# An early split of branch A's prompt columns, the sample rows' output and norm on 128 partitions, and filler matmuls in the first pauses

## The chip, the cores and the metric

The kernel runs on one core of one Trainium2 chip. A core has a matrix engine (TensorE, written PE in the profile, with its weight loads as PEld), a vector engine (VectorE, DVE), an engine for pointwise functions (ScalarE, ACT), a general engine (GpSimd, POOL) and a queue that starts transfers (SyncE, SP). The engines run side by side and wait for one another only where one needs what another makes. The time is that of the device for one execution, in microseconds (us); less is better.

## The reference

One step of a decoder layer with two gated branches, for a prompt of 512 rows and 32 sample rows (8 sequences of 4), all in float32 with 1024 features:

```python
shift, scale, gate = jnp.split(jax.nn.silu(c) @ w_cond + b_cond, 3, axis=-1)
h = x * (1 + scale[:, None]) + shift[:, None]
# one projection of h gives q, k, v, z of both branches and the two gates
ya = o_a.reshape(bsz, seq, A_OUT_WIDTH).astype(dtype) * jax.nn.silu(za)
yb = ob.reshape(bsz, seq, B_WIDTH).astype(dtype) * jax.nn.silu(zb)
merged = jax.nn.sigmoid(ga) * (ya @ w_branch_a) + jax.nn.sigmoid(gb) * (yb @ w_branch_b)
r = (ALPHA * x + gate[:, None] * (merged @ w_out)).astype(jnp.float32)
mu = jnp.mean(r, axis=-1, keepdims=True)
var = jnp.mean(jnp.square(r - mu), axis=-1, keepdims=True)
y = ((r - mu) * lax.rsqrt(var + LN_EPS)).astype(dtype) * ln_g + ln_b
```

Branch A is softmax attention over dilated windows (o_a, 512 features). Its sample rows also read 2048 cached keys and values. Branch B is a gated delta rule (o_b, 1024 features). The outputs are also the new caches and states.

## The kernel before

**Layout.** Activations are kept with features on the 128 partitions and the 544 rows (512 prompt, then 32 sample) along the free axis. A product is made in two halves of 272 columns, so the first half holds prompt rows only, and the second holds 240 prompt rows and the 32 sample rows. A float32 product is made of three fast ones: each operand is split into a rounded part (hi, an ACT copy to the type fp32r) and the rest (lo, a DVE subtraction), and hi*hi, hi*lo and lo*hi are added up in one PSUM bank.

**Order of the work.** The body doesn't issue instructions; it records them (`Recorder.add`). `Recorder.schedule` (lines 457 to 701) then makes one order for each engine: it goes through the work with a table of costs, and an engine takes the ready instruction of the lowest rank, among equals the one that was recorded first. Line 616 lets PE stay up to 1 us with matmuls of one shape before it changes to another shape that is ready. Line 625 holds an engine back from a PSUM bank until the engine that used it last is through with its work there. A field `at` keeps an instruction from being taken before that moment of the plan. `emit` (line 725) issues everything in the order found, so that every instruction of the profile carries line 725, and groups are told apart by the names of their tiles. On the chip each engine keeps its order whatever happens; a wait in it holds up all that stands behind.

**Threads.** The parts of the body are generators with ranks (lines 735 to 775). `stream` (line 1030, rank 9) runs the list `jobs` of matrix products in order; each job has its weights loaded five jobs ahead, split one job ahead, and `evac` takes each half out of PSUM. Its operations on other engines than PE get rank -1 (line 276), ahead of the rest. The samples' work has rank 1.

**Front** (lines 893 to 1017). `cond_block` (line 929) makes scale (part 1) and shift (part 0) from w_cond, for one or two of the eight 128-feature chunks: 16 narrow matmuls with `cs`, a DVE copy Y, then matmuls with the selection `selc`; both results lie in one PSUM bank. The copies x1 of the scaled input and the first three product sums (`sums`) follow chunk by chunk, as the loads of wc, xT and W3 come in.

**Before the change's middle place** (lines 2183 to 2215). The jobs are gate and branch products of B (m = 0 to 7), then the gates ga0 to ga6 (`EARLY_A` = 7). Beside them runs `samples`: the delta rule of the samples, then their attention over the cache (`sample_attention`, pieces of 128x1024 multiplied and reduced on DVE, tile `kv` into `od`; then the matmuls `pO`, lines 1847 to 1858, `om`, and a transpose into `os_`). When all threads are over, `gate_samples` (line 1875) multiplies `os_` by the gate and copies it into columns 512 to 543 of the four tiles `ya`. Lines 2224 to 2228 then split each `ya` into `yah` and `yal`. `ya` and `yah` share a tag of five buffers in the pool `keep`; `yal` takes a buffer of the tag "o" in `opool`, which has nine, and which the gates ga2 to ga6 and the eight `ybh` of branch B use as well. Then come the branch products `branch_job("ga", m)` with `merge_after(m)`, which split the merged rows into `mhi` and `mlo`. After the fourth of them w_out is loaded.

**End** (lines 2270 to 2360). For each half n of the 1024 output columns, `product_out` makes blocks tt = 0 to 3 of 128 prompt rows (24 matmuls of 512 columns; two lots of 24 with 256 columns for tt = 3). DVE takes the product out with the gate `gp`, adds the scaled x (`load_x`, two buffers) and makes the statistics `bn`. With n = 1, `norm_out` follows: aggregate, square root on ACT, three passes of `scalar_tensor_tensor` and two stores. Between the halves stands `samples_out` (line 2319): the samples' product is made with four column quarters of 256 on four groups of 32 partitions, but then brought onto partitions 0 to 31 for the addition and the norm over 1024 columns.

Of the kernel before, what the change touches and what calls it, by code (L numbers as in the profile page):

```python
# [19 lines left out]
D = 1024  # L20
# [21 lines left out]
TOGETHER = ((0,), (1, 2), (3, 4), (5, 6), (7,))  # L42
CHUNKS = ((0, 1), (1, 1), (2, 2), (4, 2), (6, 2))
# [34 lines left out]
def shape_constants():  # L78

    p = np.arange(128)  # L80
    b4, i4, h8 = p // 32, p // 8 % 4, p % 8
    blk = {}
    blk["ident"] = np.eye(128)
    blk["selc"] = (p[:, None] % 32 == np.arange(9)[None, :])
    tok = np.arange(2 * NS)
    blk["selg"] = (p[:, None] % 32 == 1 + tok[None, :] % NS // 4)
    blk["triu"] = (p[:, None] <= p[None, :])
    same = p[:, None] // 4 == p[None, :] // 4
    blk["btri"] = same & (p[:, None] <= p[None, :])
    blk["bones"] = same  # L90
    blk["low16"] = np.where(p[:, None] % 32 >= 16, -1.0, 0.0)
    blk["strict4"] = same & (p[:, None] < p[None, :])
    blk["dmask"] = np.where(p[:, None] <= p[None, :], 0.0, -BIG)
    blk["dmask_s"] = np.where(same & (p[:, None] <= p[None, :]), 0.0, -BIG)
    blk["bmask"] = (p[:, None] % 32 // 4 == np.arange(8)[None, :])
    blk["hmask"] = (p[:, None] % 4 == np.arange(4)[None, :])
    sab = np.zeros((128, 4, 4))
    for h4 in range(4):
        for g in range(2):
            sab[4 * g + h4::16, h4, g] = 1.0  # L100
            sab[8 + 4 * g + h4::16, h4, 2 + g] = 1.0
# [3 lines left out]
    for names in (("ident", "selc", "selg", "low16", "dmask"), ("selab", "sel16", "triu", "btri", "bones"),  # L105
                  ("strict4", "dmask_s", "bmask"), ("hmask",)):
# [671 lines left out]
def body(ctx, tc, io):  # L778
# [114 lines left out]
    with ExitStack() as fctx:  # L893
# [35 lines left out]
        def cond_block(part, at, m, other):  # L929

            ps, wc, w = pb_() if other else pg(), pieces[part, at], 128 * m
            rec.rank = -1
            with rec.together():
                for k in range(KT):
                    q = k % 4
                    pe.matmul(ps[32 * q:32 * q + 32, 0:w].rearrange("p (a b) -> p a b", b=128), cs[:, k, :], wc[:, :, k, :],
                              start=(k < 4), stop=(k >= 4), tile_position=(0, 32 * q))
# [3 lines left out]
            with rec.together():  # L941
                for i in range(m):
                    pe.matmul(pv[:, i, 0:9], Y[:, 128 * i:128 * i + 128], C("selc"), start=True, stop=True)
            rec.rank = 0
# [930 lines left out]
    def gate_samples():  # L1875
        ve.scalar_tensor_tensor(os_, os_, 0.5, szs, op0=OP.mult, op1=OP.mult)
        for j in range(4):
            ve.tensor_copy(ya[j][:, SEQ:], os_[:, j])
# [330 lines left out]
    jobs += [gate_job("ga", m) for m in range(EARLY_A)]  # L2209
    threads.add(finish_early(), 0)  # L2210
    threads.add(samples(), 1)
    threads.add(after_b(), 0)
    threads.add(stream(len(jobs)), 9)
# [10 lines left out]
    for j in range(4):  # L2224
        yah[j] = keep.tile([128, NT], F32R, name="yah", tag="ya", bufs=5)
        se.activation(yah[j], ya[j], AF.Copy)
        yal[j] = op.tile([128, NT], F32R, name="yal", tag="o")
        ve.tensor_sub(yal[j], ya[j], yah[j].bitcast(F32))
# [56 lines left out]
    r = [o1.tile([128, D], F32, name=f"r{tt}") for tt in range(5)]  # L2285
# [12 lines left out]
    def load_x(tt, n):  # L2298
        rows = slice(0, 128) if tt < 4 else slice(0, 32)
        xr = o2.tile([128, 512], F32, name="xr")  # L2300
        sp.dma_start(xr[rows], io["x"][128 * tt:128 * tt + 128 if tt < 4 else NT, 512 * n:512 * n + 512])
        se.activation(xr[rows], xr[rows], AF.Copy, scale=ALPHA)
        return xr[rows]

    def norm_out(tt, mv=None):
        rows = slice(0, 128) if tt < 4 else slice(0, 32)
        q = r[tt][rows]
        if mv is None:
            mv = o2.tile([128, 4], F32, name="mv")[rows]
            ve.bn_aggr(mv[:, 0:2], bn[tt][rows].rearrange("p a b -> p (a b)"))  # L2310
        se.activation(mv[:, 2:3], mv[:, 1:2], AF.Sqrt, bias=eps5[rows, 0:1])
        ve.scalar_tensor_tensor(q, q, mv[:, 0:1], lng[rows], op0=OP.subtract, op1=OP.mult)
        ve.reciprocal(mv[:, 2:3], mv[:, 2:3])
        out = io["y_p"][128 * tt:128 * tt + 128] if tt < 4 else io["y_s"]
        for w in (slice(0, 512), slice(512, 1024)):
            ve.scalar_tensor_tensor(q[:, w], q[:, w], mv[:, 2:3], lnb[rows, w], op0=OP.mult, op1=OP.add)
            sp.dma_start(out[:, w], q[:, w])

    def samples_out():
        xr = [load_x(4, n) for n in range(2)]  # L2320
# [73 lines left out]
def lay_out(x):  # L2394
# [13 lines left out]
        "const_s": CONST[3],  # L2408
        "x": rows,
# [61 lines left out]
```

## Time and profile before

| | |
|---|---|
| median of three runs | 898.17 us (897.95, 898.17, 901.1) |
| profiled execution | 902.66 us |
| its span, first to last instruction | 900.9 us |
| mean granted clock of TensorE | 0.993 |
| memory read, written | 218.20 MB, 103.97 MB |
| costliest groups | matmuls of hhi and hlo with the weights, 4080 of 128x272: 1201.5 us of (overlapping) busy time |

The profile is of one execution. A row in order of time has the start and the length in us, the engine, the operation, out<-in with partitions x elements, the count, and in brackets how long the engine had been idle before it and what ended that. A row of a group has the count, then the busy time in us and the mean of one in ns, then the idle time before. Matmuls overlap: the pace is the distance of their starts, not their length.

### The profile page before, as it was taken

Reading aid. Unit: us, or ns where it says so; the run is one execution under the profiler, and the core shown is the slowest. Engines: PE = TensorE matmul, PEld = TensorE weight load, DVE = VectorE, ACT = ScalarE, POOL = GpSimd, SP = SyncE. Lnnn points to the kernel's source line nnn. Section 1 sums busy time; section 2 is a strip of 40 time slices with the busy share of each in tenths; the row PEclk is TensorE's granted clock in tenths of the full one; section 3 lists DMA queues with packets and bytes.
Section 4 is the critical chain, followed back from the end, with each engine's and each line's share of the span. In section 5 each row is a group of like instructions: output and inputs, shape, how many; then the busy total and the mean of one; then the engine's idle time right before and its main releaser. Section 6 shows DMA issues by size and latency. Waiting matters only on the chain.

```text
span 900.9 us, 20727 instructions
## 1 busy us (share of the span) xinstructions
PE 873.6 (97%) x8178; PEld 822.2 (91%) x8178; DVE 650.8 (72%) x1341; ACT 449.9 (50%) x1076; POOL 74.1 (8%) x173
## 2 busy tenths in 40 slices
PE   6999999999999999999999999999999999989995
PEld 5899999898899999899999899897999999989884
DVE  3675447643379998399987658366889698978568
ACT  3555478733478834579734565642542222324331
POOL 0120011100101200012101101020010000001000
PEclk9999999999999999999999999999999999999998
DMA  9865785785868798878889556559869799985953
GB/s 348 322 212 172 235 277 174 249 275 165 293 200 302 234 293 276 309 245 261 274 287 286 188 193 214 177 180 317 315 224 382 270 408 411 352 305 170 366 187 122
DMA packets 106189, 235.84 MB, mean 262 GB/s; under 512 B 30199, under 2 KB 61633, under 8 KB 103405
## 3 DMA queue, kind: packets, MB, share of 16 engines
q1 hardware_dynamic: 106092, 234.53, 76.3%
q8 instruction: 64, 1.05, 0.5%
q14 instruction: 33, 0.26, 0.1%
HBM read 218.20 MB, written 103.97 MB: 358 GB/s over the span
## 4 chain that ended last, share of the span: by engine, by line
PE 83%; DVE 7%; ACT 4%; DMA 4%; issue 1%; SPq 1%; DVEq 0%; ACTq 0%
PE pp L725 63%; PE pg L725 9%; PE pd L725 7%; PE pb L725 4%; DVE slab L725 1%; ACT L725 1%; DMA S<-in_state_delta 1%; DVE lo L725 1%; DMA rbo<-dO 1%; DVE acc L725 1%; DVE r L725 1%; DMA slab<-in_bias_s 1%; SPq L725 1%; DMA out_kv_s<-in_cache 1%; DMA wc<-in_w_cb 1%
## 5 line engine op out<-in xcount | busy, mean ns | idle before, releaser
L725 PE MATMUL pp<-hhi,hi 128*128 128x272 f32 x1360 | 400.8, 295 | 1.0 <-DVE zt L725 0.5
L725 PE MATMUL pp<-hlo,hi 128*128 128x272 f32 x1360 | 400.8, 295 | 0.0
L725 PE MATMUL pp<-hhi,lo 128*128 128x272 f32 x1360 | 399.9, 294 | 0.0
L725 PEld LDWEIGHTS pp<-hhi,hi 128*128 128x128 f32 x1360 | 256.8, 189 | 4.8 <-issue 2.2
L725 PEld LDWEIGHTS pp<-hhi,lo 128*128 128x128 f32 x1360 | 256.6, 189 | 3.8 <-issue 2.7
L725 PEld LDWEIGHTS pp<-hlo,hi 128*128 128x128 f32 x1360 | 257.1, 189 | 2.8 <-issue 1.7
L725 ACT ACTIVATE hi<-wt 128x1024 fp32r<-128x1024 f32 (+1 forms) x101 | 103.6, 1026 | 160.3 <-PE pp L725 135.1
L725 DVE TENSOR_TENSOR lo<-wt,hi 128x1024 fp32r<-128x1024 f32 (+1 forms) x101 | 119.0, 1178 | 81.3 <-ACT hi L725 74.5
L725 DVE SCALAR_TENSOR_TENSOR acc<-ext,cw,acc 128x568 f32<-128x568 f32 x72 | 57.9, 804 | 0.8 <-ACT acc L725 0.2
L725 DVE TENSOR_TENSOR slab<-slab 128x512 f32<-128x512 f32 (+1 forms) x66 | 43.3, 670 | 10.0 <-DMA slab<-qd 4.4
L725 ACT ACT_TABLE_LOAD x32 | 41.1, 1283 | 5.2 <-PE pp L725 3.0
L725 DVE TENSOR_REDUCE slab<-slab 128x8 f32<-128x512 f32 (+2 forms) x66 | 42.8, 660 | 0.3
L725 ACT ACTIVATE zt<-pp 128x272 f32<-128x272 f32 x48 | 18.8, 391 | 40.6 <-PE pp L725 38.4
L725 ACT ACTIVATE P<-P,st 128x256 f32<-128x256 f32 (+1 forms) x64 | 31.3, 493 | 12.7 <-DVE st L725 12.6
L725 PE MATMUL pp<-ybh,lo 128*128 128x272 f32 x128 | 37.0, 289 | 0.0
L725 PE MATMUL pp<-ybl,hi 128*128 128x272 f32 x128 | 37.0, 289 | 0.0
L725 PE MATMUL pp<-ybh,hi 128*128 128x272 f32 x128 | 36.8, 288 | 0.0
L725 POOL COPY cx<-ext 128x3 f32<-128x3 f32 (+1 forms) x48 | 23.9, 527 | 114.5 <-ACT ext L725 109.9
L725 DVE CUSTOM_DVE_ANT_0 P<-pg,bias 128x256 f32<-128x256 f32 (+1 forms) x64 | 23.1, 401 | 9.3 <-PE pg L725 9.1
L725 ACT ACTIVATE spare<-pp 128x272 f32<-128x272 f32 (+1 forms) x32 | 16.2, 505 | 19.8 <-PE pp L725 18.2
L725 PEld LDWEIGHTS pp<-ybh,hi 128*128 128x128 f32 x128 | 24.2, 189 | 0.1
L725 PEld LDWEIGHTS pp<-ybl,hi 128*128 128x128 f32 x128 | 24.1, 188 | 0.1
(402 smaller groups left out, 1574.5 us busy)
## 6 DMA issues: line engine op xcount, KB each, us to landing
out_kv_s<-in_cache SPq DMA_DIRECT2D x144, 512.0 KB
wt<-in_w_in SPq DMA_DIRECT2D x85, 512.0 KB
out_kv_s<-in_cache SPq DMA_DIRECT2D x24, 496.0 KB
wc<-in_w_cb SPq DMA_DIRECT2D x16, 512.0 KB
slab<-in_ks SPq DMA_DIRECT2D x32, 256.0 KB
slab<-in_vs SPq DMA_DIRECT2D x32, 256.0 KB
kv<-in_ks SPq DMA_DIRECT2D x16, 512.0 KB
kv<-in_vs SPq DMA_DIRECT2D x16, 512.0 KB
```

Source lines behind the costliest of these rows:

```text
L725: getattr(real[x.engine], x.name)(*map(arg, x.args), **{k: arg(v) for k, v in x.kw.items()})
```

## The change

It has three parts, and each keeps what is computed.

- *Front.* `cond_block` of chunk 0, part 1, gets 8 matmuls of ones by ones ahead of its 16, 2 right behind them and 5 behind the selection matmuls, written to the unused columns 384 to 511 of the block's bank. The block of chunk 1 may not start before 9.9 us of the plan.
- *Middle.* A thread `split_prompt_a` of rank 0 splits columns 0 to 511 of `ya` when job `jobs[-4]` (ga3) is over, one tile every 6 us of the plan. `gate_samples` splits the 32 sample columns straight into `yah` and `yal`, with 4 ACT copies and 4 DVE subtractions of 128x32, and lines 2224 to 2228 go.
- *End.* `samples_out` keeps the four quarters on their 128 partitions: product, addition and statistics are 256 wide. The mean and the variance over the four quarters come from two matmuls with `quarter` (0.25 where two partitions hold the same row). `ln_g` and `ln_b` are loaded a second time in that layout (`lns`, eight small transfers), x and y_s are moved in four pieces each.

```diff
+IDLE = (8, 2, 5)
...
+    blk["quarter"] = np.where(p[:, None] % 32 == p[None, :] % 32, 0.25, 0.0)
...
             ps, wc, w = pb_() if other else pg(), pieces[part, at], 128 * m
+            idle = IDLE if (part, at) == (1, 0) else (0, 0, 0)
             rec.rank = -1
+
+            def turn_over(n):
+                for _ in range(n):
+                    pe.matmul(ps[:, 384:512], ones, ones, start=True, stop=True)
+
+            turn_over(idle[0])
             with rec.together():
                 for k in range(KT):
                     q = k % 4
                     pe.matmul(ps[32 * q:32 * q + 32, 0:w].rearrange("p (a b) -> p a b", b=128), cs[:, k, :], wc[:, :, k, :],
-                              start=(k < 4), stop=(k >= 4), tile_position=(0, 32 * q))
+                              start=(k < 4), stop=(k >= 4), tile_position=(0, 32 * q)).at = 9.9 * ((part, at) == (1, 1))
+                turn_over(idle[1])
...
                 for i in range(m):
                     pe.matmul(pv[:, i, 0:9], Y[:, 128 * i:128 * i + 128], C("selc"), start=True, stop=True)
+                turn_over(idle[2])
...
     def gate_samples():
         ve.scalar_tensor_tensor(os_, os_, 0.5, szs, op0=OP.mult, op1=OP.mult)
         for j in range(4):
-            ve.tensor_copy(ya[j][:, SEQ:], os_[:, j])
+            se.activation(yah[j][:, SEQ:], os_[:, j], AF.Copy)
+            ve.tensor_sub(yal[j][:, SEQ:], os_[:, j], yah[j][:, SEQ:].bitcast(F32))
+
+    def split_prompt_a():
+        yield split_at.over
+        for j in range(4):
+            yah[j] = keep.tile([128, NT], F32R, name="yah", tag="ya", bufs=5)
+            se.activation(yah[j][:, :SEQ], ya[j][:, :SEQ], AF.Copy)
+            yal[j] = op.tile([128, NT], F32R, name="yal", tag="o")
+            ve.tensor_sub(yal[j][:, :SEQ], ya[j][:, :SEQ], yah[j][:, :SEQ].bitcast(F32))
+            yield 6.0
...
     jobs += [gate_job("ga", m) for m in range(EARLY_A)]
+    split_at = jobs[-4]
     threads.add(finish_early(), 0)
     threads.add(samples(), 1)
     threads.add(after_b(), 0)
+    threads.add(split_prompt_a(), 0)
...
-    for j in range(4):
-        yah[j] = keep.tile([128, NT], F32R, name="yah", tag="ya", bufs=5)
-        se.activation(yah[j], ya[j], AF.Copy)
-        yal[j] = op.tile([128, NT], F32R, name="yal", tag="o")
-        ve.tensor_sub(yal[j], ya[j], yah[j].bitcast(F32))
...
+    lns = o1.tile([128, 2, 256], F32, name="lns")
+    for i, n in enumerate(("ln_g", "ln_b")):
+        for q in range(4):
+            sp.dma_start(lns[32 * q:32 * q + 32, i], io[n][:, 256 * q:256 * q + 256].to_broadcast([32, 256]))
+    quarter = o1.tile([128, 128], F32, name="quarter")
+    sp.dma_start(quarter, io["const_q"])
...
     def samples_out():
-        xr = [load_x(4, n) for n in range(2)]
+        xr = o1.tile([128, 256], F32, name="xs")
+        for b in range(4):
+            sp.dma_start(xr[32 * b:32 * b + 32], io["x"][SEQ:NT, 256 * b:256 * b + 256])
+        se.activation(xr, xr, AF.Copy, scale=ALPHA)
...
-        q = r[4][0:32]
+        q = r[4]
+        ve.scalar_tensor_tensor(q, po[:, 0:256], 0.5, gs, op0=OP.mult, op1=OP.mult)
+        ve.tensor_add(q, q, xr)
+        ve.bn_stats(bn[4][:, 0, :], q)
+        mv = o2.tile([128, 4], F32, name="mv")
+        ve.bn_aggr(mv[:, 0:2], bn[4][:, 0, :])
+        pm = pd()
+        pe.matmul(pm[:, 0:1], quarter, mv[:, 0:1], start=True, stop=True)
+        se.activation(mv[:, 2:3], pm[:, 0:1], AF.Square, bias=mv[:, 0:1], scale=-1.0)
+        ve.tensor_add(mv[:, 1:2], mv[:, 1:2], mv[:, 2:3])
+        pe.matmul(pm[:, 1:2], quarter, mv[:, 1:2], start=True, stop=True)
+        se.activation(mv[:, 3:4], pm[:, 1:2], AF.Sqrt, bias=eps5)
+        ve.tensor_copy(mv[:, 2:3], pm[:, 0:1])
+        ve.scalar_tensor_tensor(q, q, mv[:, 2:3], lns[:, 0], op0=OP.subtract, op1=OP.mult)
+        ve.reciprocal(mv[:, 3:4], mv[:, 3:4])
+        ve.scalar_tensor_tensor(q, q, mv[:, 3:4], lns[:, 1], op0=OP.mult, op1=OP.add)
         for b in range(4):
-            rows = slice(32 * b, 32 * b + 32)
-            ve.scalar_tensor_tensor(q[:, 256 * b:256 * b + 256], po[rows, 0:256], 0.5, gs[rows], op0=OP.mult, op1=OP.mult)
-        for n in range(2):
-            w = slice(512 * n, 512 * n + 512)
-            ve.tensor_add(q[:, w], q[:, w], xr[n])
-            ve.bn_stats(bn[4][0:32, n, :], q[:, w])
-        norm_out(4)
+            sp.dma_start(io["y_s"][:, 256 * b:256 * b + 256], q[32 * b:32 * b + 32])
```

More of the change, by code (lines that the diff above doesn't have):

```diff
@@ L105, in shape_constants @@
     for names in (("ident", "selc", "selg", "low16", "dmask"), ("selab", "sel16", "triu", "btri", "bones"),
-                  ("strict4", "dmask_s", "bmask"), ("hmask",)):
+                  ("strict4", "dmask_s", "bmask"), ("hmask",), ("quarter",)):
         at = 0
@@ L2284, in body @@
     ve.memset(eps5, LN_EPS)
-    r = [o1.tile([128, D], F32, name=f"r{tt}") for tt in range(5)]
+    lns = o1.tile([128, 2, 256], F32, name="lns")
[4 more added lines that the diff above has]
+    sp.dma_start(quarter, io["const_q"])
+    r = [o1.tile([128, D if tt < 4 else 256], F32, name=f"r{tt}") for tt in range(5)]
     bn = [o1.tile([128, 4 if tt == 3 else 2, 6], F32, name=f"bn{tt}") for tt in range(5)]
@@ L2298, in load_x @@
     def load_x(tt, n):
-        rows = slice(0, 128) if tt < 4 else slice(0, 32)
         xr = o2.tile([128, 512], F32, name="xr")
-        sp.dma_start(xr[rows], io["x"][128 * tt:128 * tt + 128 if tt < 4 else NT, 512 * n:512 * n + 512])
-        se.activation(xr[rows], xr[rows], AF.Copy, scale=ALPHA)
-        return xr[rows]
+        sp.dma_start(xr, io["x"][128 * tt:128 * tt + 128, 512 * n:512 * n + 512])
+        se.activation(xr, xr, AF.Copy, scale=ALPHA)
+        return xr
     def norm_out(tt, mv=None):
-        rows = slice(0, 128) if tt < 4 else slice(0, 32)
-        q = r[tt][rows]
+        q = r[tt]
         if mv is None:
[L2309 to L2312, printed above, removed]
+            mv = o2.tile([128, 4], F32, name="mv")
+            ve.bn_aggr(mv[:, 0:2], bn[tt].rearrange("p a b -> p (a b)"))
+        se.activation(mv[:, 2:3], mv[:, 1:2], AF.Sqrt, bias=eps5)
+        ve.scalar_tensor_tensor(q, q, mv[:, 0:1], lng, op0=OP.subtract, op1=OP.mult)
         ve.reciprocal(mv[:, 2:3], mv[:, 2:3])
-        out = io["y_p"][128 * tt:128 * tt + 128] if tt < 4 else io["y_s"]
         for w in (slice(0, 512), slice(512, 1024)):
-            ve.scalar_tensor_tensor(q[:, w], q[:, w], mv[:, 2:3], lnb[rows, w], op0=OP.mult, op1=OP.add)
-            sp.dma_start(out[:, w], q[:, w])
+            ve.scalar_tensor_tensor(q[:, w], q[:, w], mv[:, 2:3], lnb[:, w], op0=OP.mult, op1=OP.add)
+            sp.dma_start(io["y_p"][128 * tt:128 * tt + 128, w], q[:, w])
     def samples_out():
-        xr = [load_x(4, n) for n in range(2)]
+        xr = o1.tile([128, 256], F32, name="xs")
+        for b in range(4):
+            sp.dma_start(xr[32 * b:32 * b + 32], io["x"][SEQ:NT, 256 * b:256 * b + 256])
+        se.activation(xr, xr, AF.Copy, scale=ALPHA)
         po = pp()
@@ L2327, in samples_out @@
                               start=(k == 0), stop=(k == 7), tile_position=(0, 32 * q))
-        q = r[4][0:32]
-        for b in range(4):
-            rows = slice(32 * b, 32 * b + 32)
-            ve.scalar_tensor_tensor(q[:, 256 * b:256 * b + 256], po[rows, 0:256], 0.5, gs[rows], op0=OP.mult, op1=OP.mult)
-        for n in range(2):
-            w = slice(512 * n, 512 * n + 512)
-            ve.tensor_add(q[:, w], q[:, w], xr[n])
-            ve.bn_stats(bn[4][0:32, n, :], q[:, w])
-        norm_out(4)
+        q = r[4]
+        ve.scalar_tensor_tensor(q, po[:, 0:256], 0.5, gs, op0=OP.mult, op1=OP.mult)
+        ve.tensor_add(q, q, xr)
+        ve.bn_stats(bn[4][:, 0, :], q)
+        mv = o2.tile([128, 4], F32, name="mv")
+        ve.bn_aggr(mv[:, 0:2], bn[4][:, 0, :])
[9 more added lines that the diff above has]
+        ve.scalar_tensor_tensor(q, q, mv[:, 3:4], lns[:, 1], op0=OP.mult, op1=OP.add)
+        for b in range(4):
+            sp.dma_start(io["y_s"][:, 256 * b:256 * b + 256], q[32 * b:32 * b + 32])
     for n in range(2):
@@ L2408, in lay_out @@
         "const_s": CONST[3],
+        "const_q": CONST[4],
         "x": rows,
```

## The prediction

> **What bounds the kernel now.** I read the busy line and the chain's shares on the page first, then the busy times by stretch, to find where TensorE (PE) is not full, and last the rows in order of time of those stretches.
>
> ```profile
> PE 873.6 (97%) x8178; PEld 822.2 (91%) x8178; DVE 650.8 (72%) x1341; ACT 449.9 (50%) x1076; POOL 74.1 (8%) x173
> PE 83%; DVE 7%; ACT 4%; DMA 4%; issue 1%; SPq 1%; DVEq 0%; ACTq 0%
> 0.00:5.00 5.00, 0.00 (x0) 0.00 (x0) 0.89 (x6) 1.55 (x2) 0.52 (x5) 1.00 0.56 158
> 5.00:10.00 5.00, 2.60 (x34) 1.75 (x34) 1.82 (x5) 1.36 (x3) 0.00 (x0) 1.00 1.01 356
> 750.00:800.00 50.00, 50.00 (x447) 49.64 (x446) 46.99 (x50) 14.53 (x29) 0.00 (x0) 1.00 0.97 367
> 800.00:820.00 20.00, 17.14 (x127) 15.08 (x126) 12.92 (x29) 7.04 (x12) 0.82 (x2) 0.91 0.61 188
> 890.00:900.90 10.90, 0.67 (x6) 0.46 (x4) 7.63 (x15) 0.48 (x2) 0.00 (x0) 0.70 0.30 113
> ```
>
> The columns of a stretch are its length, PE, PEld, DVE, ACT, POOL, granted clock, DMA share and GB/s. PE is busy 873.6 of 900.9 us. Of the 27.3 us that it is not, 7.4 lie in the first 10 us, 2.9 in 800 to 820 and 10.2 after 890. The change works at exactly these three places; a us gained there reaches the end only if PE stays full behind it, which the shares of the chain (PE 83%) say it mostly does.
>
> **Part 1, the prompt's split.** Before, branch A's columns are split (ACT copy, then DVE subtraction, tile by tile) only after the samples' attention is over:
>
> ```profile
> 802.76 0.42 DVE L725 TENSOR_TENSOR om<-pg,od 128x256 f32<-128x256 f32 x1 [1.95 <-PE pg L725]
> 804.24 0.29 PE L725 MATMUL pp<-hhi,lo 128*128 128x272 f32 x1
> 804.67 0.29 DVE L725 TENSOR_REDUCE os__7008<-pg 128x64 f32<-128x128 f32 x1 [0.64 <-PE pg L725]
> 805.21 0.69 DVE L725 TENSOR_TENSOR lo<-wt,hi 128x512 fp32r<-128x512 f32 x1
> 806.73 0.52 PE L725 MATMUL pp<-yah,hi 128*128 128x272 f32 x2 [2.09 <-ACT yah L725]
> 807.47 0.66 ACT L725 ACTIVATE yah<-ya 128x544 fp32r<-128x544 f32 x1 [0.79 <-DVE yal L725]
> 813.16 0.39 PE L725 MATMUL pp<-yah,hi 128*128 128x272 f32 x1 [0.28 <-DVE zt L725]
> 808.00:812.00 4.00, 3.76 (x18) 3.28 (x17) 2.17 (x3) 1.44 (x3) 0.00 (x0) 0.63 0.84 272
> ```
>
> The last gate job's matmuls end at 804.36, and the second branch-A job starts at 813.16: 8.8 us for one job of 24 matmuls. In that stage of full clock such a matmul starts every 0.125 us (6.29 us for 50 in the chain's rows), so the job is worth 3.0 us and one transpose 0.1. **The excess is 5.7 us**: PE waits 2.09 for the first yah, then 1.45 us a tile for the ACT/DVE ping-pong (yah of the next tile waits for yal, 0.79, since five buffers serve ya and yah), then runs at half rate from 809 to 812 (clock 0.63 in that stretch).
>
> After the change, the first half (columns 0 to 271, prompt only) needs no sample and can run at 804.4 at once: 12 x 0.125 = 1.5 us, to 805.9. The second half waits for the 32 sample columns. That chain is os at 805.0 plus 0.29 for the gate, an ACT copy (0.22) and a DVE subtraction (0.19) of 128x32, and perhaps the weights' subtraction of 0.69 that already stands between them: first column ready at 805.7 to 806.4, the next tiles 0.2 us apart, faster than PE uses them (0.375).
>
> ```profile
> L725 ACT ACTIVATE ybh<-zbs 128x32 fp32r<-128x32 f32 x8 | 1.2, 220 | 0.4 <-DVE zbs L725 0.4
> L725 DVE TENSOR_TENSOR ybl<-zbs,ybh 128x32 fp32r<-128x32 f32 x8 | 1.0, 190 | 0.0
> L725 DVE TENSOR_TENSOR lo<-wt,hi 128x512 fp32r<-128x512 f32 x8 | 5.5, 685 | 0.0
> 799.92 0.40 ACT L725 ACTIVATE zt<-pp 128x272 f32<-128x272 f32 x1 [2.24 <-PE pp L725]
> ```
>
> What the moved work costs: four ACT copies find ACT idle 70% of 750 to 800. Four DVE subtractions of 128x512, 0.685 each (0.60 apart when back to back), land on a DVE that is 94% busy there, in front of rank-1 sample work, so od is late by up to 2.4 us. Cover: DVE waits 1.95 us for PE before om, so of three subtractions (1.8 us) that fall before the end of od, and the fourth, which waits for the buffer order behind ga6's evacuation at 799.92, only 0.5 to 0.9 comes through. If pO, which PE runs at 801.2, is late by as much as od, the cover is gone and the whole 2.4 comes through. I take 0.6, by the row of 1.95. PE then waits 0.4 to 1.2 us after 805.9 instead of losing 5.7. **Taken: 4.9 us gained**; bounds 5.7 (no wait) and 1.7 (2.4 us of delay plus 0.4 more, and 1.2 us at half rate after so long a pause). The yal tiles take four of the nine "o" buffers 20 us earlier; with ga2 to ga6 that makes nine, and the eight ybh of branch B are done by then, so no gate waits for a buffer. Behind 813, DVE needs about as long per job as PE, and the jobs and their loads shift together.
>
> **Part 2, the samples' output.** Of samples_out, DVE does on 32 partitions four products, two additions, two statistics, one 1024-wide and two 512-wide normalisations:
>
> ```profile
> L725 DVE SCALAR_TENSOR_TENSOR r<-pp,gs 32x256 f32<-32x256 f32 x4 | 1.7, 418 | 1.9 <-PE pp L725 1.8
> L725 DVE TENSOR_TENSOR r<-r,xr 32x512 f32<-32x512 f32 x2 | 1.4, 676 | 0.0
> L725 DVE BATCH_NORM_STATS2 bn<-r 32x6 f32<-32x512 f32 x2 | 1.4, 682 | 0.1
> L725 DVE SCALAR_TENSOR_TENSOR r<-r,mv,lng 32x1024 f32<-32x1024 f32 x1 | 1.3, 1273 | 0.0
> L725 DVE SCALAR_TENSOR_TENSOR r<-r,mv,lnb 32x512 f32<-32x512 f32 x2 | 1.4, 736 | 0.0
> 849.38 1.66 SPq L725 DMA_DIRECT2D xr<-in_x  x2
> 859.19 1.29 ACT L725 ACTIVATE xr<-xr 128x512 f32<-128x512 f32 x2 [2.15 <-DMA xr<-in_x]
> 865.58 0.70 DVE L725 BATCH_NORM_STATS2 bn<-r 128x6 f32<-128x512 f32 x1
> 890.38 0.29 PE L725 MATMUL pp<-wo1h,mlo 128*128 128x256 f32 x1
> 893.66 1.27 DVE L725 SCALAR_TENSOR_TENSOR r<-r,mv,lng 128x1024 f32<-128x1024 f32 x1
> 896.36 1.41 DVE L725 SCALAR_TENSOR_TENSOR r<-r,mv,lnb 128x512 f32<-128x512 f32 x2
> ```
>
> That is 7.1 us, 7.5 with an aggregate and a reciprocal. After: one product, one addition, one statistic, two normalisations, all 256 wide at 0.42, and four tiny ones at 0.15 to 0.2: 2.8. **DVE is freed of 4.7 us.** It counts because the end is DVE's: PE's last matmul ends at 890.67, DVE's last at 897.77, and of these 7.1 us 2.85 (the 1.27 at 893.66, a reciprocal, the 1.41 at 896.36) are row block 2's, left over. Its product is ready 5.8 us before PE's end (48 matmuls of 256 columns, 0.119 apart, and 0.1); DVE needs about 4.6 for it and 1.3 for block 3's first half, 5.9 in all, so with nothing left from earlier blocks 0 to 1.3 remains; I take 0.85. Gain 2.0. The price: two 1-column matmuls with full weights amid PE's stream, for which the trace has four 9-column ones in 0.51 us (17.14, quoted below); with the break, 0.2 each, 0.4. **Taken: 1.6 net**; bounds 2.85 and -0.4. The nine new loads (lns eight, quarter one), 0.4 us each on SP ahead of block 0's x, I cost at nothing: x lands 9.8 us after its trigger (849.38 to 859.19), for the transfers ahead of it, and DVE has caught up by 866.3, before 868, when PE starts the second half. The samples' x takes four triggers instead of two and y_s four instead of two, the latter long before the last y_p. Without that cover the second rival follows.
>
> **Part 3, the fillers.**
>
> ```profile
> 5.16 1.08 PE L725 MATMUL pg<-wc,cs 128*32 128x128 f32 x16 [5.16 <-DMA wc<-in_w_cb]
> 7.28 0.17 DVE L725 SCALAR_TENSOR_TENSOR sc<-pg,bT 128x9 f32<-128x9 f32 x1 [0.69 <-PE pg L725]
> 9.08 1.08 PE L725 MATMUL pb<-wc,cs 128*32 128x128 f32 x16 [1.84 <-DMA wc<-in_w_cb]
> 10.09 0.82 PE L725 MATMUL pp<-x1h,hi 128*128 128x272 f32 x2
> 13.40 0.43 PE L725 MATMUL pd<-x1h,lo 128*128 128x272 f32 x1
> 13.94 0.29 PE L725 MATMUL pg<-x1h,hi 128*128 128x272 f32 x1
> 15.16 1.07 PE L725 MATMUL pg<-wc,cs 128*32 128x256 f32 x16
> 15.18 0.84 ACT L725 ACTIVATE hi<-W 128x768 fp32r<-128x768 f32 x1 [1.82 <-DMA W<-in_w]
> 17.14 0.51 PE L725 MATMUL pg<-cst,Y 128*128 128x9 f32 x4
> 18.67 0.40 PE L725 MATMUL pp<-x1h,hi 128*128 128x272 f32 x1 [0.29 <-ACT x1h L725]
> ```
>
> The same matmul lasts 0.43 until 13.6 and 0.29 after; starts are 0.225 apart, then 0.125. With sixteen of them before 13.6, and a first block of 16 narrow ones, the slow rate costs about 2.1 us. A filler I estimate at 0.23 slow, twice the 0.11 by which the four full-weight matmuls at 17.14 follow one another: eight end by 3.1, before the load that ends PE's wait at 5.16, and cost nothing. The two behind the first block stand in its bank, and line 625 lets DVE have a bank only when PE is through with it: Y is 0.45 late. The five behind the selection hold sc back in the same way, together 1.6: 7.28 becomes 8.9, x1h's ACT copy goes from 8.11 to 9.1, and the first real matmul still comes at about 9.9, since block (1,1) (9.08 to 10.16) now stands behind it. PE is then busy from 5.2 on but for two pauses, and I expect the full rate 3.4 us sooner, near 10.2. But PE cannot keep all of it: chunk 2 starts at 18.67 because its chain hangs on W, landed at 15.18, and on block (1,2) at 15.16; from W the earliest is about 17.1. **Taken: 0.8 gained**; bounds 1.6 and -0.5 (sc late, rate unchanged).
>
> The change of rate has rows of its own: slow until 13.6, and again from 809 to 812.4. [...]
>
> **Sum.** 4.9 + 1.6 + 0.8 = 7.3 us. The profiled execution took 902.66 (span 900.9 and 1.76 around it), so 895.4; the runs' median is 898.17, 4.5 below that execution, so **890.9**. The order of everything between is planned anew, and PE's other gaps, some 5 us between 200 and 750, may move by 1 us either way.
>
> **Rivals.**
> *The samples' end slips.* DVE's 94% in 750 to 800 speaks for it, the 1.95 us before om against. Part 1 gives 3.0 down to 1.7; total 5.4 to 4.1: 892.8 to 894.1. Chance 0.18.
> *The new matmuls stop PE* (the other side). PE is in order, so the first waits for DVE's aggregate, behind it the whole second output half. PE arrives 5.7 us earlier than before, while x comes when the DMA queues bring it (9.8 us after its trigger, above), and nine more triggers stand before it, 3.7 us. If x gains nothing from PE's lead, DVE finishes the first half at 866.3 as now and the samples' chain to the aggregate (1.6) at 867.9; PE, at the place at 864.3 (868 less 5.7, and 2 us of other matmuls in between), waits 3.6, and 894.5 results; with the triggers' 3.7 in full on top it is 7.3 and 898.2. From a wait of 7.3 us the kernel is slower than before, one for one; with the second round of x (3.6 us from trigger to use) late too, 10.9, it is 901.8. Against: DVE has 1.3 us of idle before block 0's product now, and x for the samples gets a tile of its own. Chance 0.13 for 893 to 898, 0.05 beyond.
> *The change does not do it in front:* fillers only hold sc, rate turns at 13.6 as now: 1.3 worse, 892.2. Chance 0.09.
> *Forecast*, 0.55.
>
> **Numbers.** Sums of the bounds are -10.2 and -0.8, seldom all at once; the range 888.0 to 896.5 leaves about 0.1 on the high side and less on the low. About 0.5% is what measuring tells from no change, 4.5 us, so faster means below 893.7: most of the forecast's 0.55, the better part of the first rival, the front's: 0.69. Same 0.26, slower 0.05.
>
> **What would show it.** Right: yah and yal of 128x512 between 780 and 803 in DVE's rows; a first branch-A matmul within 0.3 us of the last gate matmul, a pause under 1.5 us before its second half, no stretch at half rate; after PE's last matmul about 5 us of DVE instead of 7.1; 272-wide matmuls at 0.125 from near 10. Wrong: a pause of 3 us at pp<-yah; PE waiting for DVE mv at a quarter matmul; sc after 10; x1h of chunk 2 still at 18.6.

## The result, and the profile after

The changed kernel takes 895.5 us (median of 20 runs, 893.0 to 899.29); before, in the same set, takes 900.93 (median of 20, 897.95 to 904.9). The ratio is 0.9941, 95% interval 0.9927 to 0.9955: 5.3 us faster, with 4.0 to 6.6 in the interval. A later set of runs gave 0.9937 (0.9916 to 0.9959). The forecast was 890.9, by 7.3 us below a median of three runs of 898.17. Of the 4.6 us between forecast and result, 2.8 are that starting point (twenty runs have their median at 900.93), and about 2 are expected gain that did not come.

The two profiled executions lie 8.8 us apart (spans 900.9 and 892.1), more than the medians do. Before's execution is 1.7 above its median and the changed one's 1.6 below its own, so the pair must not be read as one difference. First the busy line of the changed kernel, and its busy times in the stretch of the middle place, with the columns of the prediction:

```profile
PE 873.2 (98%) x8212; PEld 822.6 (92%) x8212; DVE 646.1 (72%) x1337; ACT 449.9 (50%) x1080; POOL 73.3 (8%) x173
800.00:820.00 20.00, 19.50 (x156) 19.31 (x155) 17.02 (x36) 8.78 (x18) 2.94 (x6) 1.00 0.63 210
```

800 to 820 has 19.50 us of PE instead of 17.14, and full clock.

**The middle.** The rows of PE, DVE and ACT in order of time:

```profile
794.52 0.68 DVE L727 TENSOR_TENSOR yal<-ya,yah 128x512 fp32r<-128x512 f32 x1
797.96 0.42 DVE L727 TENSOR_TENSOR om<-pg,od 128x256 f32<-128x256 f32 x1
799.47 0.29 PE L727 MATMUL pp<-yah,hi 128*128 128x272 f32 x1
801.29 0.59 ACT L727 ACTIVATE yah<-os__7023 128x32 fp32r<-128x32 f32 x4 [0.77 <-DVE os__7023 L727]
801.88 0.36 PE L727 MATMUL pp<-yah,hi 128*128 128x272 f32 x1 [0.49 <-ACT yah L727]
```

The last of the four 512-wide subtractions is over at 795.2; branch A's first half follows the last gate job without a pause at 799.47; the second half waits 0.49 us for the sample columns, and no stretch runs at half rate. Before, om started 1.6 us before branch A could begin (802.76 against 804.36); here it is 1.5 (797.96 against 799.47). So the four subtractions (0.6 each back to back) delay the samples by only 0.1 us against PE. The 1.95 us that om waited for PE before are gone: om now starts without a wait, so that cover took most of the subtractions' time.

**The front.** PE, DVE and ACT, in order of time:

```profile
1.05 3.78 PE L727 MATMUL pg<-ones 128*128 128x128 f32 x16 [1.05 <-DVE ones L727]
5.07 1.08 PE L727 MATMUL pg<-wc,cs 128*32 128x128 f32 x16 [0.23 <-DMA wc<-in_w_cb]
6.08 0.81 PE L727 MATMUL pg<-ones 128*128 128x128 f32 x4
7.52 1.36 PE L727 MATMUL pg<-ones 128*128 128x128 f32 x10
8.92 0.17 DVE L727 SCALAR_TENSOR_TENSOR sc<-pg,bT 128x9 f32<-128x9 f32 x1
9.89 0.52 PE L727 MATMUL pp<-x1h,hi 128*128 128x272 f32 x2
15.54 0.85 ACT L727 ACTIVATE hi<-W 128x768 fp32r<-128x768 f32 x1 [2.83 <-DMA W<-in_w]
17.08 0.36 PE L727 MATMUL pp<-x1h,hi 128*128 128x272 f32 x1
```

The eight leading fillers take 0.47 each, the last five 0.27: the rate changes in between. The trace also records when the granted clock changes, and there it is 6.31. sc comes at 8.92, the first real matmul at 9.89, at full rate, and chunk 2 starts at 17.08 instead of 18.67.

**The end.** ACT, PE and DVE of the changed kernel, around the samples' output and behind it:

```profile
859.80 0.28 PE L727 MATMUL pd<-mv,quarter 128*128 128x1 f32 x2
864.11 1.31 ACT L727 ACTIVATE xr<-xr 128x512 f32<-128x512 f32 x2 [2.16 <-DMA xr<-in_x]
864.78 1.10 DVE L727 TENSOR_TENSOR r<-r,xr 128x512 f32<-128x512 f32 x2 [0.18 <-ACT xr L727]
870.09 0.68 DVE L727 TENSOR_TENSOR r<-r,xr 128x512 f32<-128x512 f32 x1
884.49 1.27 DVE L727 SCALAR_TENSOR_TENSOR r<-r,mv,lng 128x1024 f32<-128x1024 f32 x1
887.20 1.42 DVE L727 SCALAR_TENSOR_TENSOR r<-r,mv,lnb 128x512 f32<-128x512 f32 x2
```

PE's last matmul ends at 880.72 and DVE's last product at 888.62: 7.9 us, where before had 7.1 and about 5 were forecast. Block 2's 1.27 and 1.42 still stand behind PE's end. The first half's third and fourth x only come to ACT at 864.1, and their additions wait until 864.8. The second half's first block, taken out of PSUM at 863.91, is added to its x only at 870.09. At the quarter matmul PE waits for nothing.

**One measure for all that follows.** The stretch from the moment at which PE may take branch A (the start of whatever it takes behind the last gate matmul) to the end of the span nearly repeats from one execution of a kernel to the next (92.63 and 92.77 in two of the changed kernel, 89.25 and 89.24 in two of the best version below), while the way there doesn't. In the changed kernel that is the first branch-A matmul, 799.47; to 892.1 it is 92.63. Before has a transpose in that place:

```profile
804.36 0.27 PE L725 MATMUL pg<-cst,o 128*128 128x128 f32 x1
```

From 804.36 to 900.9 it is 96.54. **Behind that point the change is worth 3.9 us.** The 8.8 of the two executions are 1.6 up to chunk 2, 3.3 between chunk 2 and branch A, and 3.9 behind; the middle 3.3 are taken up below.

### The profile page after: what moved, and what is told of

Read it like the earlier page. It is cut to its first block, busy times and chain, and to the rows that moved or that the text cites. A ratio compares the mean times of both kernels' runs of the same rounds, so it can differ in the third digit from the quotient of the medians.

```text
span 892.1 us, 20814 instructions
## 1 busy us (share of the span) xinstructions
PE 873.2 (98%) x8212; PEld 822.6 (92%) x8212; DVE 646.1 (72%) x1337; ACT 449.9 (50%) x1080; POOL 73.3 (8%) x173
## 3 DMA queue, kind: packets, MB, share of 16 engines
q8 instruction: 64, 1.05, 0.5%
## 4 chain that ended last, share of the span: by engine, by line
PE 88%; DVE 4%; ACT 3%; SPq 2%; DMA 2%; issue 1%; DVEq 0%; ACTq 0%
PE pp L727 67%; PE pg L727 10%; PE pd L727 8%; PE pb L727 4%; SPq L727 2%; DMA wc<-in_w_cb 1%; DVE r L727 1%; DMA rbo<-dO 1%; DVE lo L727 1%; ACT L727 1%; ACT sq L727 1%; DVE acc L727 1%; ACT P L727 0%; ACT hi L727 0%; DVE slab L727 0%
```

## Experiments: the parts alone

Theory A is the prediction's: split 4.9, samples' output 1.6, fillers 0.8. Theory B comes from the changed kernel's rows: split 5, samples' output nothing since x is late, fillers 1.6.

**Split alone.** Before with split_prompt_a, the new gate_samples and the removed loop.

```
+    threads.add(split_prompt_a(), 0)
...
-    for j in range(4):
-        yah[j] = keep.tile([128, NT], F32R, name="yah", tag="ya", bufs=5)
```

> Before with the prompt's split alone (Part 1); the planned order is that of before up to the rank-1 work of about 750 us, so nothing but the split and its sequels can move the time. The prediction's step: 4.9 us faster than before (bounds 1.7 to 5.7). Rival, the samples' end slips: 3.0 down to 1.7. From the rows of the changed kernel, where 8.8 us between the last gate matmul and the second branch-A job became 3.9 without half rate: 5.0, if PE stays full behind it.

Measured: 897.95 against 901.34 of before, 3.4 us faster; ratio 0.9963 (0.9947 to 0.9979).

**Samples' output alone.** Before with the new samples_out, its constants and loads.

```
+    lns = o1.tile([128, 2, 256], F32, name="lns")
+    quarter = o1.tile([128, 128], F32, name="quarter")
...
+        pe.matmul(pm[:, 0:1], quarter, mv[:, 0:1], start=True, stop=True)
```

> Before with the samples' output on 128 partitions alone (Part 2); the planned order is that of before up to the second half of the output. The prediction's step: 1.6 us faster (bounds 2.85 faster to 0.4 slower), and the rows behind PE's last matmul fall from 7.1 us to about 5. Rival, from the rows of the changed kernel, where 7.9 us lie behind PE's last matmul: DVE's freed time goes into waiting for x and for the small chain, and the time stays within 1 us of before, on either side.

Measured: 901.75 against 901.34; ratio 1.0014 (0.9996 to 1.0031), between 0.4 faster and 2.8 slower.

**Fillers alone.** Before with IDLE, turn_over and the due time of 9.9 us of block (1,1).

```
+IDLE = (8, 2, 5)
...
+            turn_over(idle[0])
```

> Before with the fillers alone (Part 3). The prediction's step: 0.8 us faster (bounds 1.6 faster to 0.5 slower), chunk 2's first matmul near 17.9 instead of 18.67. From the rows of the changed kernel, where it starts at 17.08: 1.6 faster. Rival: the front's gain is eaten by the order of what follows, planned anew, and the time is within 0.5 of before.

Measured: 899.58 against 901.34; ratio 0.9983 (0.9964 to 1.0003), 1.5 us faster with an interval that includes no gain. The fillers' rows are clearer, below.

**Split and fillers**, that is the changed kernel with before's samples_out.

> The changed kernel without the samples' output on 128 partitions: its rows, loads and operations are those of before there; the planned order up to the second output half is the changed kernel's. If the prediction's step for Part 2 holds, 1.6 us slower than the changed kernel, thus 3.7 us faster than before by the measured 5.3; if that part brings nothing, as fast as the changed kernel, 5.3 faster than before; if it costs time, more than 5.3 faster.

Measured: 896.73; ratio 0.9952 (0.9935 to 0.9969), 4.3 us faster than before. By times alone the samples' part is worth 1 us with an error larger than that. The stretch behind the start of branch A settles it. The columns are three moments of the profiled execution (branch A may start, as above; PE's last matmul ends; DVE's last instruction ends) and the differences, the last up to the end of the span:

| kernel | A may start | PE ends | DVE ends | A to PE's end | PE's end to DVE's | DVE's end to span's | all |
|---|---|---|---|---|---|---|---|
| before | 804.36 | 890.67 | 897.77 | 86.31 | 7.10 | 3.13 | 96.54 |
| split alone | 803.82 | 884.67 | 893.26 | 80.85 | 8.59 | 3.14 | 92.58 |
| samples' output alone | 803.10 | 889.54 | 897.43 | 86.44 | 7.89 | 3.47 | 97.80 |
| fillers alone | 804.06 | 890.42 | 897.52 | 86.36 | 7.10 | 3.08 | 96.54 |
| split and fillers | 803.24 | 884.08 | 892.67 | 80.84 | 8.59 | 3.13 | 92.56 |
| changed | 799.47 | 880.72 | 888.62 | 81.25 | 7.90 | 3.48 | 92.63 |

The two middle moments are the start plus the length of PE's last and of DVE's last row; the prediction shows these rows for before, and the last rows of the best version stand further down.

- The split takes 5.5 us out of PE's way (86.31 to 80.85), but the end gives 1.5 back (7.10 to 8.59). 4.0 remain, and 3.4 (1.9 to 4.8) were measured. The stretch at half clock goes with it: behind the first branch-A matmuls, all four executions without the split have one of 3.41 us (809.05 to 812.46 in before), and none of the ten with the split, those of the later sections included.
- The samples' output, with the split in place, takes 0.7 off DVE's end (8.59 to 7.90), adds 0.4 to PE (80.84 to 81.25: the two quarter matmuls, as priced) and 0.35 behind DVE's last instruction. The sum is nothing. Alone it costs 1.3 (96.54 to 97.80).
- The 0.35 stand in every kernel with that part (3.3 to 3.5 against 3.1). What causes them was not tried.

## Experiments: why the freed DVE time was lost

The busy line of the kernel with the samples' output alone:

```profile
PE 873.0 (97%) x8182; PEld 821.5 (91%) x8182; DVE 646.0 (72%) x1337; ACT 449.0 (50%) x1076; POOL 74.1 (8%) x173
```

DVE has 646.0 us of work there against before's 650.8: 4.8 us are gone, about as counted. The question is why the end didn't see it. Three candidates: the nine new triggers ahead of x, the two buffers of x, and DVE's amount of work itself.

**Eight buffers for x** in the changed kernel:

```
-        xr = o2.tile([128, 512], F32, name="xr")
+        xr = o2.tile([128, 512], F32, name="xr", bufs=8)
```

> The changed kernel with eight buffers for x (xr) instead of two, so that each of the eight loads of 128x512 can be triggered without waiting for an addition; order and count of all else are left to the planner. In the changed kernel 7.9 us of DVE lie behind PE's last matmul, of which 4.6 are row block 3's own and 3.3 are left over from block 2. Theory, x comes late: the rows of block 0 and 1 move into DVE's pauses of 856 to 870, the left-over goes, 4.7 to 5.5 us remain behind PE's end, and the kernel is 2.4 to 3.2 faster than the changed kernel, thus about 8 below before. Rival, DVE's own amount of work is the bound, or the small chain of the samples holds it: 7 us or more remain, and the time is within 1 us of the changed kernel, about 5 below before.

**The nine loads recorded behind the first output half**, two buffers as before the edit:

```
         if n:
+            for i, name in enumerate(("ln_g", "ln_b")):
+                for q in range(4):
+                    sp.dma_start(lns[32 * q:32 * q + 32, i], io[name][:, 256 * q:256 * q + 256].to_broadcast([32, 256]))
+            sp.dma_start(quarter, io["const_q"])
             samples_out()
```

> The changed kernel with the nine loads of lns and quarter recorded behind the first output half, so that the first half's x is triggered ahead of them; two buffers for x as in the changed kernel. Theory, the nine triggers ahead of x are what ate the freed time: the first xr is triggered 3.7 us or more sooner, the rows behind PE's last matmul fall from 7.9 to 5 to 6, and 2 us or more are gained on the changed kernel (7 below before). Rival, the two buffers hold x, whichever loads stand ahead: the third x still waits for the first addition, at least 7 us remain, and at most 1 us is gained.

**Split and fillers with eight buffers**, and **before with eight buffers**, the same one-line edit:

> The changed kernel without the samples' output on 128 partitions (the samples' rows of before), but with eight buffers for x. It says what that part is worth once x is in time. By the prediction's step, 1.6 us slower than the changed kernel with eight buffers (bounds 2.85 slower to 0.4 faster): 6.4 below before if that one is 8 below. Rival, DVE has room for the samples' 7.5 us as soon as x is in time, and the two quarter matmuls only cost PE 0.4: equal, or 0.4 faster than with that part.

> Before with eight buffers for x and nothing else. The prediction said that DVE has caught up before the second output half in before, so that x is no matter there. If so: within 0.7 us of before, and 7.1 us behind PE's last matmul as in before. Rival, x is late in before too: the left-over of block 2 (2.85 us) goes, 4.3 to 5.5 remain behind PE's end, and 1.6 to 2.8 us are gained.

Measured (before in this set 900.15):

| kernel | median us | ratio, 95% | PE's end to DVE's | A to span's end |
|---|---|---|---|---|
| changed, eight buffers | 894.43 | 0.9932 (0.9906 to 0.9959) | 4.88 | 89.69 |
| changed, nine loads later | 894.21 | 0.9937 (0.9915 to 0.9959) | 5.40 | 90.17 |
| split and fillers, eight buffers | 893.37 | 0.9931 (0.9911 to 0.9951) | 5.34 | 89.25 |
| before, eight buffers | 898.67 | 0.9984 (0.9972 to 0.9997) | 5.27 | 94.31 |

In each of them the left-over of block 2 goes (7.9 to 4.9 or 5.4; 8.6 to 5.3; 7.1 to 5.3), and the stretch gets 2.2 to 3.3 us shorter. So it is x that holds up the end, by its triggers or its buffers. That holds for before too: the forecast that its x is no matter was wrong by 2.2 us of that stretch (96.54 to 94.31), 1.4 by the ratio. The medians of the first two rows show less than the stretch (about 1 us instead of 2.5 to 2.9, against the changed kernel's 895.5 of an earlier set); the intervals of six runs are wide enough for both. For these two kernels the gain over the changed kernel rests on the stretch alone; for the best version it is measured again on one chip, last below.

SP's DMA issues show how the two remedies work. First the changed kernel, then the one with eight buffers:

```profile
839.96 3.96 SPq L727 DMA_DIRECT2D lns<-in_ln_g  x4
845.67 4.25 SPq L727 DMA_DIRECT2D lns<-in_ln_b  x4
850.43 0.90 SPq L727 DMA_DIRECT2D xr<-in_x  x2
853.25 2.42 SPq L727 DMA_DIRECT2D out_kv_s<-in_cache  x4
855.76 1.22 SPq L727 DMA_DIRECT2D xr<-in_x  x2
865.50 6.95 SPq L727 DMA_DIRECT2D xr<-in_x  x4
```

```profile
855.96 1.85 SPq L727 DMA_DIRECT2D xr<-in_x  x4
859.72 2.53 SPq L727 DMA_DIRECT2D xr<-in_x  x4
862.29 4.22 SPq L727 DMA_DIRECT2D out_kv_s<-in_cache  x5
```

The second execution reached branch A 4.1 us later (803.61 against 799.47); less that, its first x is triggered at 851.8, 1.4 later than in the changed kernel. So a late first x is not the harm. The harm is in the other six: with two buffers the third may only be triggered when an addition has freed a buffer, at 855.76, and by then SP has put four copies of 512 KB of the cache ahead of it. They are 2.1 MB at the 277 GB/s of that stretch (row below), 7.6 us, and ACT gets that x at 864.1, 8.3 after the trigger. The four of the second half follow from 865.5 to 872.5. The first of these four, triggered at 865.50 without such copies ahead of it, is at ACT by 868.35, 2.9 later. With eight buffers all eight are on their way before these copies. That x lands behind the copies is read from these two times, 8.3 us with four copies ahead and 2.9 with none; the copies alone were not moved.

The nine triggers matter through the same chain. Moved behind the first pair, they let it be triggered at 842.0 in an execution that reached branch A at 801.23; the buffers come free earlier, and the third and fourth x go out at 855.5 and 856.4, ahead of four copies:

```profile
855.51 0.37 SPq L727 DMA_DIRECT2D xr<-in_x  x1
856.86 2.41 SPq L727 DMA_DIRECT2D out_kv_s<-in_cache  x4
```

Either remedy breaks the chain. Each of them also lets the planner order the end anew, with x expected sooner. What x's arrival is worth in an unchanged order was not tried.

DVE's busy time by stretch, the changed kernel and the best kernel (split, fillers, eight buffers), columns as above:

```profile
850.00:864.00 14.00, 14.00 (x129) 11.19 (x128) 6.51 (x17) 3.49 (x6) 0.00 (x0) 1.00 0.83 277
864.00:870.00 6.00, 6.00 (x28) 4.85 (x27) 3.90 (x8) 1.90 (x3) 0.00 (x0) 1.00 0.33 114
870.00:880.00 10.00, 10.00 (x66) 9.08 (x65) 9.45 (x19) 2.38 (x5) 0.00 (x0) 1.00 0.33 110
```

```profile
850.00:864.00 14.00, 14.00 (x127) 11.12 (x126) 12.17 (x24) 7.45 (x12) 0.00 (x0) 1.00 0.80 284
864.00:870.00 6.00, 6.00 (x28) 4.87 (x27) 5.89 (x11) 0.29 (x1) 0.00 (x0) 1.00 0.09 22
870.00:880.00 10.00, 10.00 (x67) 9.12 (x66) 9.69 (x18) 0.59 (x2) 0.00 (x0) 1.00 0.28 105
```

Both executions start branch A at nearly the same time (799.47 and 799.56). From 850 to 870 the changed kernel's DVE does 10.4 us of work, the other's 18.1. Of the difference 4.8 are the wider samples' work of before, which the other kernel still has; the remaining 2.9 are work that the changed kernel does later, and its DVE ends 2.9 later (888.62 against 885.69). From 870 on both are full. The freed 4.8 us lay in a stretch in which DVE had nothing to do; work that was late, not work that was much, made the end. It also answers what the samples' part is worth once x is in time: less than nothing, 89.69 with it and 89.25 without. PE's part is 0.6 longer with it, DVE's 0.5 shorter, and the stretch behind DVE's end 0.3 longer (one execution with it, two without).

## Experiments: the front, and the best version

> The changed kernel with no filler, but with the due time of 9.9 us of block (1,1), which lets the first real matmuls go ahead of it. If the full rate in front is the fillers' work, the 272-wide matmuls stay at 0.225 us until 13.5 to 14.2, as in the four executions without fillers, and chunk 2 starts at 18.6 to 19.3. If it is the order, chunk 2 starts at 16.5 to 17.1, as in the six executions with fillers.

> The changed kernel without the eight fillers ahead of the first block; the two and the five behind it stay. If the eight are needed for the rate, the first block and the two run slow (1.08 and 1.11 us), the full rate comes at 8.6 us or later instead of 5.0 to 7.2, and chunk 2 starts 0.3 to 1 us later than 16.5 to 17.1. If seven are enough, chunk 2 starts in 16.5 to 17.1.

Edits: IDLE = (0, 0, 0) and IDLE = (0, 2, 5) in the changed kernel, one execution of each. Their rows up to the first real matmuls, the kernel without fillers first:

```profile
8.60 0.60 PE L727 MATMUL pp<-x1h,hi 128*128 128x272 f32 x1 [1.59 <-ACT x1h L727]
14.13 0.43 PE L727 MATMUL pg<-x1l,hi 128*128 128x272 f32 x1
19.82 0.39 PE L727 MATMUL pp<-x1h,hi 128*128 128x272 f32 x1
```

```profile
7.99 2.48 PE L727 MATMUL pg<-ones 128*128 128x128 f32 x10
10.40 0.88 PE L727 MATMUL pb<-wc,cs 128*32 128x128 f32 x16
11.49 0.52 PE L727 MATMUL pp<-x1h,hi 128*128 128x272 f32 x2 [0.21 <-ACT x1h L727]
18.03 0.29 PE L727 MATMUL pp<-x1h,hi 128*128 128x272 f32 x1
```

Without fillers the order alone lets the first real matmul start at 8.60, 1.3 us sooner than in the changed kernel, yet at half rate (0.43 until 14.13; the clock's record turns at 15.14), and chunk 2 starts at 19.82. With the last seven fillers the rate changes at 10.93 by the clock's record, within block (1,1) (0.88, between 1.08 slow and 0.65 fast), and chunk 2 starts at 18.03. Over all profiled executions chunk 2 starts

- without fillers or due time (four): 18.59, 18.67, 19.27, 19.28, mean 18.95;
- with all fifteen fillers (eight): 16.21 to 17.08, mean 16.68.

**The fillers gain 2.3 us up to chunk 2**, by the rate, not by the order: in the new order without fillers chunk 2 starts at 19.82, later than in the old one (one execution). The eight leading fillers are needed for 1.3 of it (one execution).

What stops the gain there is PE's own work. The rows show no pause of PE from block (1,2), the scale of chunks 2 and 3, up to chunk 2, and chunk 2 starts 3.82 us behind that block, which waits for its load wc. The changed kernel (chunk 2 at 17.08), then the best one:

```profile
13.26 1.07 PE L727 MATMUL pg<-wc,cs 128*32 128x256 f32 x16 [0.47 <-DMA wc<-in_w_cb]
```

```profile
12.39 1.07 PE L726 MATMUL pg<-wc,cs 128*32 128x256 f32 x16 [0.25 <-DMA wc<-in_w_cb]
16.21 0.39 PE L726 MATMUL pp<-x1h,hi 128*128 128x272 f32 x1
```

The chain that hangs on the load of W would be the next limit: ACT takes W at 15.54 and 14.70 and is through with chunk 2's x1h at 17.00 and 16.16, less than 0.1 us ahead of PE.

Last, the changed kernel once more, beside the best version that the runs point to: split, fillers and eight buffers for x, with the samples' rows of before.

> The changed kernel once more, on the same chip as the next, to set the two side by side: about 0.994 of before, as measured first. From the first branch-A matmul to the end of the span 92.6 us as in its first profile, if that stretch is the same in each execution; in front of it some us more or less, if the pauses between 200 and 800 cost more in some executions than in others.

> The kernel of the earlier run with the split, the fillers, eight buffers for x and the samples' rows of before, again, beside the changed kernel. From the rows, 89.3 us from the first branch-A matmul to the end of the span against 92.6 in the changed kernel: 3.3 us faster than the changed kernel. Rival, by the medians of the earlier calls, 893.4 against 895.5 over different chips: 2 us or less, and by chance nothing.

Measured on one chip (before 901.3): changed 894.9, ratio 0.9937 (0.9916 to 0.9959); best 891.68, ratio 0.9907 (0.9888 to 0.9927). From the start of branch A to the end: 92.77 and 89.24. **The best version is 3.2 us faster than the changed kernel by the medians (the six times of each allow 0.8 to 5.1), 3.5 by that stretch, and 8.4 (6.6 to 10.1) faster than before.** Its last rows:

```profile
880.12 0.29 PE L726 MATMUL pp<-wo1h,mlo 128*128 128x256 f32 x1
881.21 0.42 DVE L726 SCALAR_TENSOR_TENSOR r<-pp,gp 128x256 f32<-128x256 f32 x1
884.28 1.41 DVE L726 SCALAR_TENSOR_TENSOR r<-r,mv,lnb 128x512 f32<-128x512 f32 x2
```

PE ends at 880.41, DVE at 885.69: 5.3 us, of which the last 4.5, from the product of block 3's last 256 columns at 881.21 on, are that block's own.

## Why the prediction was right or wrong

**Part 1** named the mechanism, and its size was near: 4.9 forecast, 5.5 at PE, 4.0 at the end of the span. The samples' delay was taken as 0.6 and is 0.1; the pause was put at 0.4 to 1.2 and is 0.49. That no half-rate stretch follows and that first branch-A and last gate matmul touch came as written. What the step lacked is the end: "the jobs and their loads shift together" is not so, since 1.5 of the 5.5 are given back there. With the split alone PE ends 6.0 us sooner (890.67 to 884.67), but ACT gets the first half's x only 4.0 sooner (859.19 to 855.15). With eight buffers the 1.5 come back, and more (8.59 to 5.34).

**Part 2** failed: 1.6 forecast, nothing measured, 1.3 lost when it stands alone. DVE was freed of 4.8 us, about as counted, and the matmuls cost the 0.4 that were priced. The step that failed is the one on the nine loads, "I cost at nothing: x lands 9.8 us after its trigger", with its "DVE has caught up by 866.3, before 868", and so "Gain 2.0". The row used there shows that x is late; it was taken as cover for more triggers, when it was the sign that DVE's end hangs on x. The nine triggers, priced at 3.7 us, held SP from 839.96 to 850.39, 10.4 us. Two buffers tie each later x to an addition, and the additions to the x before. And with x in time (eight buffers) the rewritten samples' work gains only 0.5 behind PE's end, not 2.0, since DVE then has room for the wide work too. The rival with the late x had the right cause in the wrong place: PE did not wait for the aggregate (no wait stands at the quarter matmuls), DVE had pauses instead and was late at the end.

**Part 3** had the mechanism right and the size too small: 0.8 forecast, bounds 1.6 and -0.5; 1.6 in the profiled pair, 2.3 over twelve executions, above the bound, 1.5 by the ratio of the run with the fillers alone. Three terms were off. Slow fillers take 0.47 each, not 0.23, and still end before the first load. The full rate comes at 4.9 to 7.2, not near 10.2: before's record has it at 13.75, so it came 6.5 to 8.8 us sooner, and no run shows the 3.4 us of the forecast. And chunk 2 came 1.5 behind W's load, held by PE's own work, so the 1.9 in "from W the earliest is about 17.1" was too long by at least 0.4. The row sc, forecast at 8.9, came at 8.92.

**The sum.** By the measure that repeats, 2.3 + 3.9 = 6.2 are gained; 5.3 (4.0 to 6.6) were measured, 7.3 were forecast. That the sum came this near is in part luck: part 2 lacks 1.7 and part 1 lacks 0.9 at the end, while part 3 brings 1.5 more than forecast.

**The way between.** That PE's other gaps "may move by 1 us either way" was too little for one execution, and the new order is not the reason. From chunk 2 to branch A the changed kernel's plan took 782.39 us in its first profiled execution and 786.80 in the one with eight buffers, whose order on PE is the same up to there. Of these 4.4 us, 3.2 come between the same matmuls near 490 and 510: in the second execution PE pauses for 2.20 us and then has half the clock for 3.41.

```profile
495.02:498.43 3.41, 1.21 (x32) 0.94 (x30) 2.20 (x6) 0.63 (x1) 1.23 (x2) 1.00 0.87 350
498.43:501.85 3.42, 3.42 (x33) 1.63 (x34) 0.22 (x1) 0.75 (x2) 0.00 (x0) 0.50 0.36 150
```

Over the executions that were averaged for chunk 2, the way takes 784.6 us in the mean of the four without fillers and 784.7 in the mean of the eight with them, so the order planned anew costs and gains nothing. What tells them apart is the clock: four of the twelve have such a stretch of 3.41 us at half clock on the way, before's own among them, and took 785.7 to 787.3; the eight without one took 782.1 to 784.6. So the profiled pair alone would have credited the change with 3.3 us that belong to the moment.

## What to carry to other kernels

Before freeing an engine at the end of a kernel, look at what it waits for in the stretch where the time would come free: if its inputs are late there, the freed time becomes idle time (here 4.8 us of DVE), and an earlier trigger or more buffers for those inputs is worth more (here 3.3 us for one number, against nothing for the rewritten arithmetic). Count with each load which buffer must come free first and which large copies its queue will then have ahead of it (here 2.1 MB, and x 8.3 us behind its trigger instead of 2.9). And judge a change of half a per cent by landmarks that repeat, such as the time from one known matmul to the end (here 92.63 and 92.77 in two executions), since the whole times of one and the same program (893.0 to 899.29 in twenty runs of the changed kernel) differ by as much as the change brings.

## What the runs showed of the hardware

The moment at which the rate rises (from matmuls 0.225 us apart to 0.125) moves with the execution. With the same fifteen fillers, busy from 1.05 on, the nine-column products at 6.6 to 7.6 were fast (0.39 for two, 0.60 when slow) in all eight executions, but the first block of weights was slow in four of them (1.08) and fast in four (0.65 to 0.69). The earliest change and the latest, the best kernel and the changed kernel's second profile:

```profile
4.94 0.65 PE L726 MATMUL pg<-wc,cs 128*32 128x128 f32 x16
```

```profile
4.87 1.08 PE L727 MATMUL pg<-wc,cs 128*32 128x128 f32 x16
5.88 1.22 PE L727 MATMUL pg<-ones 128*128 128x128 f32 x4
```

By the clock's records the change lies at 4.93 in the one and at 7.24 in the other, and the rows agree: in the one the first block is fast from 4.94 on, in the other the two fillers behind it are slow up to 7.10 and the nine-column products at 7.49 are fast. The eight leading fillers take 3.78 us, and with them the rate was up by 7.56 in each of the eight executions. With the last seven alone, behind a first block at 4.93, it rose at 10.93. With none and the first real matmul at 8.60 it rose at 15.14, in the block of 14.49, which took 1.36 us (1.07 at the full rate); in before at 13.75. So work of PE ahead brought the change sooner in these runs; what sets its moment within them was not shown.

A pause can cost more than its length, and not each time. In the execution with eight buffers, the pause of 2.20 us lies whole within one stretch of 3.41 us, and the next 3.41 us have half the clock (rows above). The changed kernel has pauses of about the same sum near 620, but they are spread over two such stretches (0.80 and 1.02 us), and the clock stays at 1.00:

```profile
617.30:620.71 3.41, 2.61 (x88) 2.33 (x80) 1.11 (x1) 0.00 (x0) 0.29 (x1) 1.00 0.92 277
620.71:624.12 3.41, 2.39 (x18) 1.96 (x17) 1.51 (x3) 0.00 (x0) 0.00 (x0) 1.00 1.07 329
```

The stretches are counted from the moments at which the clock changes in the same execution. In before's record these are 13.75, 242.44, 245.85, 809.05, 812.46 and 894.38, which lie 67, 1, 165, 1 and 24 times 3.413 us apart; in the changed kernel's they are 6.31 and 883.54, 257 times 3.413 us apart. In the fourteen profiled executions the clock falls eight times between chunk 2 and the last matmuls, each time for 3.41 us. In the 3.41 us ahead of the fall PE was busy for 2.07 and 1.84 us in before (0.61 and 0.54 of the time; the falls at 242.44 and 809.05) and for 1.21 us in the execution with eight buffers (0.35). Of the other stretches of before and of the changed kernel, from the first change to PE's last matmul, the least busy have 2.39 us (0.70), and the clock fell behind none of them. So in these executions a pause was dear where it fell into one such stretch, and where the stretches begin differs from one execution to the next.
